# One fp32 encoder step on one core: the sample group's attention as a pipeline, and the first tiles of x, the key buffers and the last output projection in another order

## The chip, the cores and the metric

The kernel runs on one core of a Trainium2 chip. A core has a matrix engine (TensorE, PE in the profile, with PEld for its weight loads), VectorE (DVE), ScalarE (ACT), GpSimd (POOL) and SyncE (SP), which here issues every DMA. Each engine works off its own instructions strictly in the order in which they were put. The metric is the device time of one execution in microseconds (us), and a kernel's time is the median of its runs.

## The reference

17 tiles of 128 tokens go through one layer: 16 tiles of a prompt of 2048 tokens, and one tile that holds the sample group, 8 sequences of 16 new tokens with a cache of 1024 keys and values each. Everything is fp32.

```python
h = rms_norm(x, norm_g[l])
(a_x, a_b, a_c, a_z, g_q, g_f, g_i, g_z,
 s_q, s_k, s_v, s_z, m_a, m_b, m_c) = split_cols(h @ w_in[l])   # 1024 -> 15 column segments
...                      # A: gated 3-tap convolution; B: gated linear recurrence in chunks
q = rms_norm(s_q.reshape(B, T, 8, 64), q_norm_g[l])             # C: stick-breaking attention
k = rms_norm(s_k.reshape(B, T, 8, 64), k_norm_g[l])
k_all = concat([past_k, k]); v_all = concat([past_v, v])        # sample group; the prompt has no past
z = einsum('bqhd,bkhd->bhqk', q, k_all) / sqrt(64)
log_1mb = where(causal, log_sigmoid(-z), 0.0)
rest = cumsum(log_1mb, axis=3, reverse=True) - log_1mb          # from the newest key back
A = where(causal, exp(log_sigmoid(z) + rest), 0.0)
o = einsum('bhqk,bkhd->bqhd', A, v_all)
...
m = sigmoid(m_a) * (o_a @ wb[:512]) + sigmoid(m_b) * (o_b @ wb[512:1024]) + sigmoid(m_c) * (o_c @ wb[1024:])
y = x + m @ w_out[l]
```

## The kernel before

**Arithmetic.** Each fp32 operand of a large product is split into a high and a low part (`split`: a rounding cast `hi` on ACT, and `lo = src - hi` on DVE), and each product takes three matmuls, hi·hi, hi·lo and lo·hi (`PASS3`). `wload` fetches 512 KB of weights at a time into `wst` (two buffers) and splits them into `whi` and `wlo`.

**Head.** Before the first projection `first_steps` loads five tiles of x; tile 0 is the sample group. For each, ACT squares and sums a row (`square`, L505), POOL makes the reciprocal root (`rstd_of`: `rv` L195, `rr` L197), DVE scales by it and by the gain row `g_bc` (`scale`, L510), PE transposes in two halves of four 128x128 blocks (`turn`, L521), and each half is split into `hh` and `hl`. The first projection needs tiles 0 to 2. POOL also builds constants there: `qblk` and `bsel`, and the masks `mtmp`, which DVE casts into `lmask`.

**Projections.** The tiles are taken in three groups. For each, `run_jobs` walks a list of jobs, one for each weight slice; a job is a generator, and after every few matmuls it yields a cost and lets queues of other work go on by so much: `run_late` (the end of `post_qk`), `hbg` (the recurrence) and `bg`. `post_qk` takes q or k of a tile, norms it, transposes it (L700) and copies it to `kt` (L702), which one DMA writes to `KT` or `QT`; `kt` has one buffer.

**The sample group's attention** runs in `bg` during the second group, from some 624 to 1231 us. For each of 8 sequences and three segments of keys (`sg` 2, 1, 0, newest first), 24 steps in all, it loads cached keys `kc`, transposes them into `kt`, multiplies by the zero-padded queries `qz` (`z`, L412), takes two sigmoids on ACT, a scan and a product `sp` on DVE (L426), transposes `sp` on PE (L429), copies that to `at_` on ACT (L436) and multiplies it by the cached values `vc` into `pv` (L447). One step ends before the next begins. The newest segment has two cached blocks and 16 new keys, which go a path of their own.

**Prompt attention** follows in `bg` from the third group on.

**Merge.** From some 2290 us on, groups of tiles (`PGROUPS`) go through `bjob(x, dp)` for the three branches (matmuls L1225; `gate` L1233 on DVE; from the second branch on the sum `mp` on POOL, L1234; after the third `mp` is split into `mh` and `ml`), and `ojob(s)` multiplies by four slices of `w_out` (L1247) and adds x (`yt`, L1253). The output jobs of a group are put between the next group's branch jobs. The last group has four tiles, and its four output jobs have nothing left beside them.

Rows of the profile name a line, an engine, an operation, and the tiles written and read, so "L429 tp<-idf,sp" is the transposition of `sp` at line 429.

Of the kernel before, what the change touches and what calls it, by code (L numbers as in the profile page):

```python
# [16 lines left out]
P = 128  # L17
# [81 lines left out]
def trunk(ctx: ExitStack, tc: tile.TileContext, x_prompt, x_sample, cache_conv, state_hgrn, cache_k, cache_v,  # L99
# [72 lines left out]
    nc.sync.dma_start(g_bc, norm_g[0].partition_broadcast(P))  # L172

    def split(hi, lo, src, eng=None):

        nc.scalar.copy(hi, src)  # L176
        (eng or nc.vector).tensor_tensor(lo, src, hi.bitcast(F32), ALU.subtract)  # L177

    def wload(pieces):

        out = []
        for v in pieces:
            a, b = v.shape[1], v.shape[2]
            st = wp.tile([P, a, b], F32, tag="wst", name="wst", bufs=2)
            nc.sync.dma_start(st, v)
            hi = wp.tile([P, a, b], F32R, tag="whi", name="whi")
            lo = wp.tile([P, a, b], F32R, tag="wlo", name="wlo")
            split(hi, lo, st)
            out.append((hi, lo))
        return out  # L190

    def rstd_of(ssq, n, count):
# [4 lines left out]
        nc.gpsimd.tensor_tensor(r, v, mhalf.broadcast_to([P, n]), ALU.pow)  # L197
        return r
# [58 lines left out]
    def attn_pair(m0, m1):  # L257
# [15 lines left out]
        for m in range(m0, m1):  # L273
# [8 lines left out]
            for i in range(nq):  # L282
# [17 lines left out]
                if b0 > 0:  # L300
                    carry[e][i] = at.tile([P, 1], F32, tag="carry", name="carry", bufs=16)
# [42 lines left out]
    def sample_attention():  # L344
# [45 lines left out]
        for b in range(NB):  # L390
            pv = ps_pv()
            carry = one
            vnew = sa.tile([TS, 8, 64], F32, tag="vnew", name="vnew", bufs=1)
            nc.sync.dma_start(vnew, VV[b * TS:(b + 1) * TS])
            for sg in (2, 1, 0):
                nblk = 2 if sg == 2 else 3
                w = nblk * P + (TS if sg == 2 else 0)
                kt = sa.tile([P, 4, 384], F32, tag="kt", name="kt", bufs=2)
                for bi in range(nblk):
                    blk = 3 * sg + bi  # L400
                    kc = sa.tile([P, 512], F32, tag="cst", name="kc", bufs=3)
                    nc.sync.dma_start(kc, cache_k[0, b, blk * P:(blk + 1) * P].rearrange("t h d -> t (h d)"))
                    tp = ps_tp()
                    for h in range(4):
                        nc.tensor.transpose(tp[:, h * P:(h + 1) * P], kc[:, h * P:(h + 1) * P], idf)
                    nc.scalar.copy(kt[:, :, bi * P:(bi + 1) * P], tp.rearrange("p (h t) -> p h t", h=4))
                    yield 1.3
                z = ps_z()
                if sg == 2:
                    nc.tensor.matmul(z[:, 256:256 + TS], idb, nmask, start=True, stop=False, skip_group_check=True)  # L410
                for h in range(4):
                    nc.tensor.matmul(z[32 * h:32 * h + 32, :nblk * P], qz[:, h, b], kt[:, h, :nblk * P],  # L412
                                     start=sg != 2, stop=True, skip_group_check=True)
                if sg == 2:
                    for h in range(4):
                        nc.tensor.matmul(z[32 * h:32 * h + 32, 256:256 + TS], qz[:, h, b],
                                         knew[:, h, b * TS:(b + 1) * TS], start=False, stop=True,
                                         skip_group_check=True)
                nc.scalar.activation(sn[:, 384 - w:384], z[:, :w], AF.Sigmoid, scale=-0.125)
                sp = sa.tile([P, 384], F32, tag="sp", name="sp")  # L420
                nc.scalar.activation(sp[:, :w], z[:, :w], AF.Sigmoid, scale=0.125)
                pr = sa.tile([P, 385], F32, tag="pr", name="pr")
                s_in = sn[:, 384 - w:385][:, ::-1]
                nc.vector.tensor_tensor_scan(pr[:, 384 - w:385][:, ::-1], s_in, s_in, carry, ALU.mult, ALU.bypass)
                carry = pr[:, 384 - w:385 - w]
                nc.vector.tensor_tensor(sp[:, :w], sp[:, :w], pr[:, 385 - w:385], ALU.mult)  # L426
                tp = ps_tp()
                for bi in range(nblk):
                    nc.tensor.transpose(tp[:, bi * P:(bi + 1) * P], sp[:, bi * P:(bi + 1) * P], idf)  # L429
                at_ = sa.tile([P, 384], F32, tag="at", name="at_")  # L430
                if sg == 2:
                    nc.tensor.transpose(tp[0:TS, 256:384], sp[:, 256:256 + TS], idf)
                    nc.scalar.copy(at_[:, 0:256], tp[:, 0:256])
                    nc.scalar.copy(at_[0:TS, 256:384], tp[0:TS, 256:384])
                else:
                    nc.scalar.copy(at_, tp[:, :384])  # L436
                yield 2.0
                for bi in range(3):
                    blk = 3 * sg + bi
                    if blk == 8:  # L440
                        vc, n = vnew, TS
                    else:
                        vc, n = sa.tile([P, 8, 64], F32, tag="vst", name="vc", bufs=3), P
                        nc.sync.dma_start(vc, cache_v[0, b, blk * P:(blk + 1) * P])
                    for h in range(4):
                        c = bi * P + 32 * h
                        nc.tensor.matmul(pv[32 * h:32 * h + 32, 0:P].rearrange("p (e d) -> p e d", e=2),  # L447
                                         at_[0:n, c:c + 32], vc[0:n, 2 * h:2 * h + 2],
                                         start=sg == 2 and bi == 0, stop=sg == 0 and bi == 2, skip_group_check=True)
                    yield 0.6  # L450
            od = sa.tile([P, P], F32, tag="od", name="od", bufs=1)
            nc.scalar.copy(od, pv[:, 0:P])
            for h in range(8):
                nc.sync.dma_start(OCS[b * TS:(b + 1) * TS, h * 64:(h + 1) * 64],
                                  od[h * TS:(h + 1) * TS, 64 * (h % 2):64 * (h % 2) + 64])
            yield 1.0
# [24 lines left out]
    class Prepare:  # L481
# [30 lines left out]
        def turn(self, i, kk):  # L512
# [10 lines left out]
            split(hh[sl], hl[sl], tp.rearrange("p (k t) -> p k t", k=4))  # L523
# [42 lines left out]

# [74 lines left out]
    lmax = const.tile([P, 4], F32, name="lmax")  # L641
    nc.vector.tensor_copy(lmax, vec[:, 12:16])
    lexp = const.tile([P, 4], F32, name="lexp")
    nc.vector.tensor_tensor(lexp, vec[:, 12:16], lmax, ALU.subtract)
    ebase = const.tile([P, 1], F32, name="ebase")
    nc.vector.memset(ebase, 2.718281828459045)
    nc.gpsimd.tensor_tensor(lexp, ebase.broadcast_to([P, 4]), lexp, ALU.pow)
    lsum = const.tile([P, 4], F32, name="lsum")
    nc.vector.reciprocal(lsum, lexp)
    lsm = const.tile([P, 4], F32, name="lsm")  # L650
    nc.vector.tensor_tensor(lsm, lexp, lsum, ALU.mult)
    lb = const.tile([P, 4], F32, name="lb")
    nc.vector.tensor_tensor(lb, lsm, lsm, ALU.subtract)
    omlb = const.tile([P, 4], F32, name="omlb")
    nc.vector.tensor_scalar(omlb, lb, -1.0, 1.0, ALU.mult, ALU.add)
# [4 lines left out]
    for h in (1, 2, 4, 8, 16, 32, 64):  # L660
        nblk = 64 // h
        mt = g0p.tile([P, 2, 64], F32, tag="mtmp", name="mtmp", bufs=2)
        nc.gpsimd.memset(mt[:, :, :nblk], 1.0)
        for i in range(2):
            m = mt[:, i, :nblk]
            nc.gpsimd.affine_select(m, m, pattern=[[-2 * h, nblk]], base=-h * i, channel_multiplier=1,
                                    compare_op=ALU.is_ge, fill=0.0)
            nc.gpsimd.affine_select(m, m, pattern=[[2 * h, nblk]], base=h + h * i, channel_multiplier=-1,
                                    compare_op=ALU.is_gt, fill=0.0)
        lmask[h] = const.tile([P, 2 * nblk], I32, name=f"lmask{h}")  # L670
        nc.vector.tensor_copy(lmask[h].rearrange("p (i b) -> p i b", i=2), mt[:, :, :nblk])
# [632 lines left out]
```

## Time and profile before

| | |
|---|---|
| runs | median 3031.82 us (3031.12 to 3034.32, 3 runs) |
| profiled execution | 3036.76 us; its span on the core 3035.1 us |
| TensorE clock granted, mean | 0.991 of full speed |
| PE matmuls | 2934.7 us, 97% of the span, 19609 instructions |
| DVE | 1759.2 us, 58% |
| ACT | 1230.2 us, 41% |
| POOL | 454.7 us, 15% |
| DMA | 394.40 MB, 130 GB/s |

The profile shows one execution; its own time is 4.94 us above the median, so differences are worked out against 3036.76 and the result is carried to the median. PE is busy nearly throughout, and what is left on it is idle gaps and stretches where the clock of its matmuls is granted at half speed.

### The profile page before, as it was taken

How to read it: one execution, taken by the hardware profiler on the slowest of the kernel's cores; microseconds unless marked ns; L12 is line 12 of the kernel's file. 1: busy time of each engine (PE TensorE's matmuls, PEld its weight loads, DVE VectorE, ACT ScalarE, POOL GpSimd, SP SyncE). 2: the span in 40 equal slices, each digit the busy share in tenths (PEclk: the TensorE clock that was granted, in tenths of full speed). 3: DMA queues.
4: the chain of work that ended last, by engine and by line, in shares of the span. 5: the costliest groups of instructions: out<-in, count | busy, mean ns of one | idle time of the engine just before them, and what ended most of it. 6: DMA issues, size and time to landing. Idle time of an engine off the chain costs nothing. (4 is left out here: it accounts for less than half of the span.)

```text
span 3035.1 us, 51813 instructions
## 1 busy us (share of the span) xinstructions
PE 2934.7 (97%) x19609; PEld 2688.3 (89%) x19609; DVE 1759.2 (58%) x3412; ACT 1230.2 (41%) x2571; POOL 454.7 (15%) x861
## 2 busy tenths in 40 slices
PE   7999999999999999999999999999999899899998
PEld 7999999988988888999899998998998788687887
DVE  5345535652434352636635757567577877978753
ACT  4332232243333333224434444444445555555531
POOL 3110000110100000001322111111012412313211
PEclk9999999999999999999999999999999999999999
DMA  5433323455444444323444232323226455555553
GB/s 178 139 109 112 99 90 105 120 161 166 130 126 138 130 131 121 115 78 114 150 152 127 81 122 81 119 66 100 89 87 216 149 164 171 157 184 170 171 160 121
DMA packets 448842, 394.40 MB, mean 130 GB/s; under 512 B 24809, under 2 KB 388674, under 8 KB 448594
## 3 DMA queue, kind: packets, MB, share of 16 engines
q1 hardware_dynamic: 448594, 391.09, 42.3%
q8 instruction: 155, 2.54, 0.4%
q14 instruction: 93, 0.76, 0.1%
HBM read 303.67 MB, written 87.33 MB: 129 GB/s over the span
## 5 line engine op out<-in xcount | busy, mean ns | idle before, releaser
L587 PE MATMUL acc<-hh,whi 128*128 128x384 f32 (+1 forms) x2688 | 937.8, 349 | 0.5 <-ACT hh L176 0.3
L587 PE MATMUL acc<-hl,whi 128*128 128x384 f32 (+1 forms) x2688 | 887.6, 330 | 0.0
L587 PE MATMUL acc<-hh,wlo 128*128 128x384 f32 (+1 forms) x2688 | 887.5, 330 | 0.0
L177 DVE TENSOR_TENSOR wlo<-wst,whi 128x1024 fp32r<-128x1024 f32 x296 | 372.1, 1260 | 435.0 <-ACT whi L176 420.7
L587 PEld LDWEIGHTS acc<-hh,whi 128*128 128x128 f32 x2688 | 508.1, 189 | 37.3 <-issue 31.1
L587 PEld LDWEIGHTS acc<-hl,whi 128*128 128x128 f32 x2688 | 509.2, 189 | 4.9 <-issue 1.0
L587 PEld LDWEIGHTS acc<-hh,wlo 128*128 128x128 f32 x2688 | 507.3, 189 | 0.0
L176 ACT CAST whi<-wst 128x1024 fp32r<-128x1024 f32 x296 | 311.0, 1051 | 364.1 <-PE acc L587 272.4
L598 PE MATMUL acc<-whi,hh 128*128 128x256 f32 x1088 | 317.2, 292 | 7.2 <-DVE gm L986 5.0
L598 PE MATMUL acc<-wlo,hh 128*128 128x256 f32 x1088 | 308.6, 284 | 0.5 <-DVE wlo L177 0.5
L598 PE MATMUL acc<-whi,hl 128*128 128x256 f32 x1088 | 308.6, 284 | 0.0
L298 DVE TENSOR_TENSOR_SCAN pr<-snb,carry 128x513 f32<-128x513 f32 x192 | 259.4, 1352 | 74.3 <-ACT snb L289 73.2
L271 ACT COPY aT<-tp 128x512 f32<-128x512 f32 (+2 forms) x320 | 167.8, 525 | 236.3 <-PE tp L270 233.6
L303 DVE TENSOR_TENSOR sp<-sp,pr 128x512 f32<-128x512 f32 (+2 forms) x320 | 202.0, 631 | 35.1 <-POOL sp L294 13.2
L598 PEld LDWEIGHTS acc<-whi,hh 128*128 128x128 f32 x1088 | 207.2, 190 | 11.7 <-DVE gm L986 5.7
L289 ACT ACTIVATE snb<-z 128x512 f32<-128x512 f32 (+2 forms) x320 | 172.3, 539 | 90.2 <-PE z L286 85.5
L598 PEld LDWEIGHTS acc<-wlo,hh 128*128 128x128 f32 x1088 | 207.4, 191 | 0.7 <-DVE wlo L177 0.7
L598 PEld LDWEIGHTS acc<-whi,hl 128*128 128x128 f32 x1088 | 207.4, 191 | 0.4
L270 PE MATMUL tp<-idf,sp 128*128 128x128 f32 x1088 | 173.1, 275 | 15.8 <-ACT aT L271 15.1
L1225 PE MATMUL acc<-oh,whi 128*128 128x512 f32 (+2 forms) x480 | 179.8, 376 | 8.6 <-DVE gate L1233 7.1
L298 DVE TENSOR_TENSOR_SCAN pr<-snb,one 128x129 f32<-128x129 f32 (+3 forms) x128 | 114.5, 894 | 112.1 <-POOL snb L294 112.0
L291 ACT ACTIVATE sp<-z 128x512 f32<-128x512 f32 (+2 forms) x320 | 171.7, 537 | 16.9 <-DMA OX<-ot 13.0
(301 smaller groups left out, 4773.4 us busy)
## 6 DMA issues: line engine op xcount, KB each, us to landing
wst<-in_w_in_dram SPq DMA_DIRECT2D x216, 512.0 KB, 3.9
wst<-in_w_branch_dram SPq DMA_DIRECT2D x48, 512.0 KB, 4.0
GM<-gm SPq DMA_DIRECT2D x120, 192.0 KB, 2.0
Kt<-KT SPq DMA_DIRECT2D x80, 256.0 KB, 3.1
gate<-GM SPq DMA_DIRECT2D x72, 256.0 KB, 2.7
kc<-in_cache_k_dram SPq DMA_DIRECT2D x64, 256.0 KB, 2.9
vc<-in_cache_v_dram SPq DMA_DIRECT2D x64, 256.0 KB, 2.8
wst<-in_w_out_dram SPq DMA_DIRECT2D x32, 512.0 KB, 4.5
```

The source lines that it names most:

```text
L176: nc.scalar.copy(hi, src)
L177: (eng or nc.vector).tensor_tensor(lo, src, hi.bitcast(F32), ALU.subtract)
L270: nc.tensor.transpose(tp[:, j * P:(j + 1) * P], sp[:, j * P:(j + 1) * P], idf)
L271: nc.scalar.copy(aT[:, e, 0:nb, i * P:(i + 1) * P], tp[:, :w].rearrange("p (b q) -> p b q", q=P))
L289: nc.scalar.activation(sn[:, 512 - w:512], z[:, :w], AF.Sigmoid, scale=-0.125)
L291: nc.scalar.activation(sp[:, :w], z[:, :w], AF.Sigmoid, scale=0.125)
L298: nc.vector.tensor_tensor_scan(pr[:, 512 - w:513][:, ::-1], s_in, s_in, one if diag else carry[e][i], ALU.mult, ALU.bypass)
L303: nc.vector.tensor_tensor(sp[:, :w], sp[:, :w], pr[:, 513 - w:513], ALU.mult)
L587: nc.tensor.matmul(acc[:, :n], w[0][a][:, k], hT[b][:, k, :n], start=k == 0 and i == 0, stop=k == KB - 1 and i == 2)
L598: nc.tensor.matmul(acc[:, :256], hT[b][:, k, ti * P:(ti + 1) * P], w[k // 4][a][:, k % 4], start=k == 0 and i == 0, stop=k == KB - 1 and i ...
L1225: nc.tensor.matmul(acc[:, :n], w[0][a][:, k, dd * P:(dd + 1) * P], box[x][b][:, k, sl], start=k == 0 and i == 0, stop=k == 3 and i == 2)
```

## The change

- `first_steps`: `g_bc` is loaded behind the sample tile. Tiles 0 to 2 are squared, scaled and transposed, and tiles 3 and 4 only behind the first split of weights. The constants (`build_bound`, `build_masks`, `build_selectors`) are put behind the latest `rr` and the first split.
- `post_qk`: `kt` has two buffers. `carry` of the prompt attention has 9 in place of 16.
- `sample_attention`: the same arithmetic, with the next step's keys transposed ahead of this step's `turned` (transposition of the product), and the next step's scores put behind this step's `values`. Two zeroed buffers `sps` and a zeroed `vnew` of 128 partitions let all steps make three transpositions and one copy. The loads of `vc` are issued in `turned`, ahead of the job's next matmuls.
- The last group's merge: for the third branch the sum `mp` is made on DVE, and the first output job takes three tiles together, first with k 0 to 5 and then with k 6 and 7. `xr` has 3 buffers, `yt` 2.

```diff
 first_steps:
+                if i == 0:
+                    nc.sync.dma_start(g_bc, norm_g[0].partition_broadcast(P))
             for f in (self.square, self.scale):
                 for i in range(2):
                     f(i)
             for i in range(n):
                 if i > 2:
-                    self.square(i)
-                    yield
-                    self.scale(i)
-                    yield
+                    with tc.issue_after(first_split[0].ins), tc.issue_after(first_split[1].ins):
+                        self.square(i)
+                        yield
+                        self.scale(i)
+                        yield
                 for kk in range(0, KB, 4):
                     self.turn(i, kk)
                     yield
-                    if i == 0:
-                        (self.scale if kk else self.square)(2)
+                    if i == 0 and not kk:
+                        self.square(2)
+                if i == 0:
+                    with tc.issue_after(self.last[1].ins):
+                        self.scale(2)
                 self.ready = i
+                yield
 run_jobs:
+            if not g and at_ == 1:
+                with tc.issue_after(rstd_at[0].ins), tc.issue_after(first_split[1].ins):
+                    build_bound()
+                    build_masks()
+                    build_selectors()
 post_qk:
-        kt = qk.tile([P, 4, P], F32R, tag="kt", name="kt", bufs=1)
+        kt = qk.tile([P, 4, P], F32R, tag="kt", name="kt", bufs=2)
 sample_attention (after):
+        sps = [single([P, 384], F32, f"sps{i}") for i in range(2)]
+        for x in sps:
+            nc.gpsimd.memset(x, 0.0)
...
+        def turned(m):
+            b, sg = order[m]
+            sp = held[m][0]
+            tp = ps_tp()
+            for bi in range(3):
+                nc.tensor.transpose(tp[:, bi * P:(bi + 1) * P], sp[:, bi * P:(bi + 1) * P], idf)
+            at_ = sa.tile([P, 384], F32, tag="at", name="at_")
+            nc.scalar.copy(at_, tp[:, :384])
+            for bi in range(blocks(m)):
+                vc = sa.tile([P, 8, 64], F32, tag="vst", name="vc", bufs=3)
+                nc.sync.dma_start(vc, cache_v[0, b, blk * P:(blk + 1) * P])
...
+        yield from keys(0)
+        scores(0, masked(0))
+        yield 0.7
+        for m in range(last + 1):
+            if m < last:
+                yield from keys(m + 1)
+            turned(m)
+            yield 2.0
+            z = masked(m + 1) if m < last else None
+            values(m)
+            if z is not None:
+                scores(m + 1, z)
+            yield 2.2
 bjob:
-                            nc.gpsimd.tensor_tensor(m, m, gate[:, sl], ALU.add)
+                            (nc.vector if final and x == 2 else nc.gpsimd).tensor_tensor(
+                                m, m, gate[:, sl], ALU.add)
 ojob:
+            cuts = [KB - 2, KB] if final and s == 0 else [KB]
...
+                    for c, end in enumerate(cuts):
+                        for ti in some:
...
+                            for k in range(cuts[c - 1] if c else 0, end):
```

What the change moves is seen in the instructions of each engine. The first place is DVE at the start of the program. Before (`xt` with numbers are x tiles 2, 3 and 4):

```order
L510 SCALAR_TENSOR_TENSOR xt<-xt,rr,g_bc 128x1024 x2
L510 SCALAR_TENSOR_TENSOR xt_119<-xt_119,rr,g_bc 128x1024
L177 TENSOR_TENSOR hl<-tp,hh 128x4x128
L671 CAST lmask_233<-mtmp 128x128
L510 SCALAR_TENSOR_TENSOR xt_121<-xt_121,rr,g_bc 128x1024
L177 TENSOR_TENSOR hl<-tp,hh 128x4x128 x2
L671 CAST lmask_241<-mtmp 128x64
L510 SCALAR_TENSOR_TENSOR xt_123<-xt_123,rr,g_bc 128x1024
L177 TENSOR_TENSOR hl<-tp,hh 128x4x128 x2
L671 CAST lmask_249<-mtmp 128x32
L177 TENSOR_TENSOR wlo<-wst,whi 128x1024
```

After:

```order
L562 SCALAR_TENSOR_TENSOR xt<-xt,rr,g_bc 128x1024 x2
L176 TENSOR_TENSOR hl<-tp,hh 128x4x128 x2
L562 SCALAR_TENSOR_TENSOR xt_119<-xt_119,rr,g_bc 128x1024
L176 TENSOR_TENSOR hl<-tp,hh 128x4x128 x4
L694 COPY vec<-tp 128x17
L176 TENSOR_TENSOR wlo<-wst,whi 128x1024
L707 COPY lmax<-vec 128x4
L711 MEMSET ebase 128x1
L562 SCALAR_TENSOR_TENSOR xt_121<-xt_121,rr,g_bc 128x1024
L176 TENSOR_TENSOR wlo<-wst,whi 128x1024
L562 SCALAR_TENSOR_TENSOR xt_123<-xt_123,rr,g_bc 128x1024
```

Ahead of the first `wlo` there stood five scalings and three casts of masks; now there stand three scalings and no cast.

The second place is PE in one step of the sample group's attention, between the scores `z` and the transposition of their product. Before, with projections (L587) and `post_qk` (L700):

```order
L412 MATMUL z<-kt,qz 32x384 x4
L587 MATMUL acc<-hh,whi 128x384
L587 MATMUL acc<-hl,whi 128x384
L587 MATMUL acc<-hh,wlo 128x384
L587 MATMUL acc<-hh,whi 128x384
L587 MATMUL acc<-hl,whi 128x384
L587 MATMUL acc<-hh,wlo 128x384
L700 MATMUL hg<-idr,st 128x128 x4
L587 MATMUL acc<-hh,whi 128x384
L587 MATMUL acc<-hl,whi 128x384
L587 MATMUL acc<-hh,wlo 128x384
L429 MATMUL tp<-idf,sp 128x128 x3
```

After, the same engine where one step's values and the next one's scores meet:

```order
L648 MATMUL acc<-hh,wlo 128x384
L429 LDWEIGHTS idb
L429 MATMUL z<-nmask,idb 128x16
L484 MATMUL pv<-vc,at__8071 32x128 x12
L438 MATMUL z<-kt,qz 32x256 x4
L442 MATMUL z<-knew,qz 32x16 x4
L648 MATMUL acc<-hh,whi 128x384
```

Nine projection matmuls and one transposition stood between `z` and its `tp`; now the scores stand behind the step before's values, and the keys of the step after, with the work of their yields, follow ahead of `tp`: the scores `z` at position 4329 of PE's order have their `tp` (L461) at position 4438, 108 rows on.

The third place is DVE at the end of the last merge group. Before:

```order
L1233 TENSOR_TENSOR gate<-acc,gate 128x512
L177 TENSOR_TENSOR ml<-mp,mh 128x512
L1233 TENSOR_TENSOR gate<-acc,gate 128x512
L177 TENSOR_TENSOR wlo<-wst,whi 128x1024
L177 TENSOR_TENSOR ml<-mp,mh 128x512
L1253 TENSOR_TENSOR yt<-acc,xr 128x256 x3
```

After:

```order
L1308 TENSOR_TENSOR gate<-acc,gate 128x512 x2
L1309 TENSOR_TENSOR mp<-mp,gate 128x512 x2
L176 TENSOR_TENSOR ml<-mp,mh 128x512 x2
L176 TENSOR_TENSOR wlo<-wst,whi 128x1024
L1308 TENSOR_TENSOR gate<-acc,gate 128x512
L1309 TENSOR_TENSOR mp<-mp,gate 128x512
L176 TENSOR_TENSOR ml<-mp,mh 128x512
L1340 TENSOR_TENSOR yt<-acc,xr 128x256 x3
```

The sums `mp` have come into DVE's order, between `gate` and `ml`; eight of them leave POOL's.

More of the change, by code (lines that the diff above doesn't have):

```diff
@@ L171, in trunk @@
     g_bc = const.tile([P, D], F32, name="g_bc")
-    nc.sync.dma_start(g_bc, norm_g[0].partition_broadcast(P))
     def split(hi, lo, src, eng=None):
-        nc.scalar.copy(hi, src)
-        (eng or nc.vector).tensor_tensor(lo, src, hi.bitcast(F32), ALU.subtract)
+        first = nc.scalar.copy(hi, src)
+        return first, (eng or nc.vector).tensor_tensor(lo, src, hi.bitcast(F32), ALU.subtract)
+    first_split = []
     def wload(pieces):
@@ L187, in wload @@
             lo = wp.tile([P, a, b], F32R, tag="wlo", name="wlo")
-            split(hi, lo, st)
+            pair = split(hi, lo, st)
+            if not first_split:
+                first_split.extend(pair)
             out.append((hi, lo))
         return out
+    rstd_at = [None]
     def rstd_of(ssq, n, count):
@@ L389, in sample_attention @@
         yield 1.0
[L390 to L410, printed above, removed]
-                for h in range(4):
[L412 to L456, printed above, removed]
@@ new lines, in sample_attention, with blocks, keys @@
+        order = [(b, sg) for b in range(NB) for sg in (2, 1, 0)]
+        held = {}
+        pvs = {}
+        sps = [single([P, 384], F32, f"sps{i}") for i in range(2)]
+        for x in sps:
+            nc.gpsimd.memset(x, 0.0)
+        vnew = single([P, 8, 64], F32, "vnew")
+        nc.gpsimd.memset(vnew, 0.0)
+        def blocks(m):
+            return 2 if order[m][1] == 2 else 3
+        def keys(m):
+            b, sg = order[m]
+            kt = sa.tile([P, 4, 384], F32, tag="kt", name="kt", bufs=2)
+            for bi in range(blocks(m)):
+                blk = 3 * sg + bi
+                kc = sa.tile([P, 512], F32, tag="cst", name="kc", bufs=3)
+                nc.sync.dma_start(kc, cache_k[0, b, blk * P:(blk + 1) * P].rearrange("t h d -> t (h d)"))
+                tp = ps_tp()
+                for h in range(4):
+                    nc.tensor.transpose(tp[:, h * P:(h + 1) * P], kc[:, h * P:(h + 1) * P], idf)
+                nc.scalar.copy(kt[:, :, bi * P:(bi + 1) * P], tp.rearrange("p (h t) -> p h t", h=4))
+                yield 1.3
+            held[m] = [kt]
@@ new lines, in masked, with scores @@
+        def masked(m):
+            z = ps_z()
+            if order[m][1] == 2:
+                nc.tensor.matmul(z[:, 256:256 + TS], idb, nmask, start=True, stop=False, skip_group_check=True)
+            return z
+        def scores(m, z):
+            b, sg = order[m]
+            nblk = blocks(m)
+            w = nblk * P + (TS if sg == 2 else 0)
+            kt = held[m][0]
+            for h in range(4):
+                nc.tensor.matmul(z[32 * h:32 * h + 32, :nblk * P], qz[:, h, b], kt[:, h, :nblk * P],
+                                 start=sg != 2, stop=True, skip_group_check=True)
+            if sg == 2:
+                for h in range(4):
+                    nc.tensor.matmul(z[32 * h:32 * h + 32, 256:256 + TS], qz[:, h, b],
+                                     knew[:, h, b * TS:(b + 1) * TS], start=False, stop=True,
+                                     skip_group_check=True)
+            nc.scalar.activation(sn[:, 384 - w:384], z[:, :w], AF.Sigmoid, scale=-0.125)
+            sp = sps[m % 2]
+            nc.scalar.activation(sp[:, :w], z[:, :w], AF.Sigmoid, scale=0.125)
+            pr = sa.tile([P, 385], F32, tag="pr", name="pr")
+            s_in = sn[:, 384 - w:385][:, ::-1]
+            carry = one if sg == 2 else held[m - 1][1]
+            nc.vector.tensor_tensor_scan(pr[:, 384 - w:385][:, ::-1], s_in, s_in, carry, ALU.mult, ALU.bypass)
+            nc.vector.tensor_tensor(sp[:, :w], sp[:, :w], pr[:, 385 - w:385], ALU.mult)
+            held[m] = [sp, pr[:, 384 - w:385 - w]]
@@ new lines, in values @@
+        def values(m):
+            b, sg = order[m]
+            at_, vs = held[m][2:4]
+            if sg == 2:
+                pvs[b] = ps_pv()
+            pv = pvs[b]
+            for bi, vc in enumerate(vs):
+                for h in range(4):
+                    c = bi * P + 32 * h
+                    nc.tensor.matmul(pv[32 * h:32 * h + 32, 0:P].rearrange("p (e d) -> p e d", e=2),
+                                     at_[:, c:c + 32], vc[:, 2 * h:2 * h + 2],
+                                     start=sg == 2 and bi == 0, stop=sg == 0 and bi == 2, skip_group_check=True)
+            if sg == 0:
+                od = sa.tile([P, P], F32, tag="od", name="od", bufs=1)
+                nc.scalar.copy(od, pv[:, 0:P])
+                for h in range(8):
+                    nc.sync.dma_start(OCS[b * TS:(b + 1) * TS, h * 64:(h + 1) * 64],
+                                      od[h * TS:(h + 1) * TS, 64 * (h % 2):64 * (h % 2) + 64])
@@ L457, in sample_attention @@
+        last = len(order) - 1
+        yield from keys(0)
[11 more added lines that the diff above has]
+            yield 2.2
         oc = sa.tile([P, 512], F32, tag="cst", name="oc", bufs=3)
@@ L522, in turn @@
             sl = (slice(None), slice(kk, kk + 4), slice(ti * P, (ti + 1) * P))
-            split(hh[sl], hl[sl], tp.rearrange("p (k t) -> p k t", k=4))
+            self.last = split(hh[sl], hl[sl], tp.rearrange("p (k t) -> p k t", k=4))
         def steps(self):
@@ new lines, in trunk, with build_masks @@
+    lmask = {}
+    def build_masks():
+        for h in (1, 2, 4, 8, 16, 32, 64):
+            nblk = 64 // h
+            mt = g0p.tile([P, 2, 64], F32, tag="mtmp", name="mtmp", bufs=2)
+            nc.gpsimd.memset(mt[:, :, :nblk], 1.0)
+            for i in range(2):
+                m = mt[:, i, :nblk]
+                nc.gpsimd.affine_select(m, m, pattern=[[-2 * h, nblk]], base=-h * i, channel_multiplier=1,
+                                        compare_op=ALU.is_ge, fill=0.0)
+                nc.gpsimd.affine_select(m, m, pattern=[[2 * h, nblk]], base=h + h * i, channel_multiplier=-1,
+                                        compare_op=ALU.is_gt, fill=0.0)
+            lmask[h] = const.tile([P, 2 * nblk], I32, name=f"lmask{h}")
+            nc.vector.tensor_copy(lmask[h].rearrange("p (i b) -> p i b", i=2), mt[:, :, :nblk])
```

100 lines of the change are left out of this document (53 added, 47 removed).

## The prediction

> **What bounds the kernel now.** I read the page first, then PE's waits, then the stretches of half clock, and then the trace at each place that the change touches. The page gives the bound.
>
> ```profile
> span 3035.1 us, 51813 instructions
> PE 2934.7 (97%) x19609; PEld 2688.3 (89%) x19609; DVE 1759.2 (58%) x3412; ACT 1230.2 (41%) x2571; POOL 454.7 (15%) x861
> ```
>
> PE is idle for 3035.1 - 2934.7 = 100.4 us. No matmul is taken away, so the change can win part of these 100 us, and of the time that matmuls lose at half clock. PE's waits, with the tile that PE was to work on and what it waited for (total us, count, longest), name the gaps:
>
> ```profile
> PE tp L521 <- DVE xt L510: 12.5, 3, 10.9
> PE tp L429 <- DVE sp L426: 11.0, 21, 2.3
> PE hg L700 <- ACT kt L702: 7.4, 6, 2.3
> PE acc L1247 <- ACT mh L176: 5.7, 3, 2.7
> PE pv L447 <- ACT at__7899 L436: 1.0, 1, 1.0
> ```
>
> The first is the head, the second and fifth are the sample group's attention, the third is `post_qk`, the fourth is the end. Next come windows around stretches of half clock. The columns are the window, its length, busy time and count of PE, PEld, DVE, ACT and POOL, the granted clock, and the share and GB/s of the DMAs. The last row is the end, at full clock.
>
> ```profile
> 69.30:76.10 6.80, 5.80 (x29) 5.80 (x29) 2.32 (x6) 1.89 (x6) 1.20 (x2) 0.50 0.67 193
> 670.00:673.40 3.40, 3.40 (x15) 3.16 (x13) 1.09 (x3) 1.56 (x3) 0.00 (x0) 0.50 0.53 174
> 707.60:711.00 3.40, 2.68 (x9) 2.17 (x7) 0.43 (x2) 0.78 (x2) 0.00 (x0) 0.50 0.54 182
> 810.00:813.40 3.40, 3.40 (x18) 3.40 (x18) 0.42 (x1) 1.10 (x3) 0.19 (x1) 0.50 0.79 230
> 1509.70:1513.10 3.40, 3.22 (x14) 3.22 (x15) 1.24 (x4) 0.82 (x5) 0.54 (x2) 0.50 0.93 280
> 1639.40:1642.80 3.40, 3.40 (x17) 3.22 (x16) 0.24 (x1) 1.68 (x5) 0.54 (x2) 0.50 0.35 114
> 2980.80:2991.10 10.30, 7.20 (x30) 6.60 (x31) 3.54 (x5) 1.76 (x3) 2.11 (x1) 0.50 0.26 78
> 2991.10:3031.20 40.10, 40.10 (x338) 39.93 (x337) 11.71 (x19) 5.25 (x5) 0.00 (x0) 1.00 0.40 128
> ```
>
> At full clock a 256-wide matmul takes 40.10 / 338 = 0.119 us. In the first window 29 of them took 5.80 us, where 3.44 would have done. A half-clock stretch so loses 41% of its busy time.
>
> **Part 1, the key buffer.** With one `kt`, the next copy waits until the DMA has written the last one out. ACT's queue stands meanwhile, and behind it the casts and evacuations that PE wants:
>
> ```profile
> 68.91 0.59 ACT L702 CAST kt<-tp 128x512 fp32r<-128x512 f32 x1 [2.98 <-DMA KT<-kt]
> 70.30 0.58 PE L598 MATMUL acc<-whi,hh 128*128 128x256 f32 x1 [2.89 <-DVE gm L986]
> PE acc L598 <- DVE gm L986: 4.0, 2, 2.9
> PE acc L598 <- ACT vg L1054: 1.0, 1, 1.0
> PE hg L700 <- ACT kt L702: 1.3, 2, 0.8
> PE hg L700 <- ACT kt L702: 6.1, 4, 2.3
> ```
>
> The last four rows are PE's waits in 50 to 200 us (two rows), 624 to 1231 and 1420 to 1660. At 70.30 the profile names `gm`, which DVE makes after ACT, and ACT had just stood 2.98 us for the write of `kt`; so I count these rows to `kt`. Idle: 4.0 + 1.0 + 1.3 + 6.1 = 12.4 us. Clock, in the windows at 69, 1509 and 1639: (5.80 + 3.22 + 3.40) x 0.41 = 5.1 us. With two buffers a copy waits only for the write before last. **17.5 us**. Bounds: 6.1 if only the waits that name `kt` in the third group go, 17.5 if all go. I take the upper end, since the waits come where two copies stand close together. What is late next is the third copy of a row of three, 0 to 3 us, which is in the allowance below.
>
> **Part 2, the sample group's attention.** Before, a step's `z` and the transposition of its product stand nine projection matmuls and one transposition apart, and PE arrives first:
>
> ```profile
> 663.64 0.85 PE L412 MATMUL z<-kt,qz 128*32 128x384 f32 x8
> 669.51 0.55 PE L429 MATMUL tp<-idf,sp 128*128 128x128 f32 x3 [2.35 <-DVE sp L426]
> ```
>
> Nine 384-wide matmuls are 9 x 0.119 x 1.5 = 1.6 us, against a chain of two sigmoids, a scan and a product. After, some hundred matmuls stand between them where I counted, over 12 us at these prices, against the same chain; even the smallest distance that I found there, about 5 us, exceeds what was 2.35 us short. All of 11.0 + 1.0 = 12.0 us idle should go, and the half-clock stretches that follow these gaps: (3.40 + 2.68 + 3.40) x 0.41 = 3.9 us. **15.9 us**, bounds 10 (a third of the waits stay) and 20 (the grouped `pv` and `z` matmuls, some 4 us of further small gaps). The instructions added cost PE nothing: 8 sequences lose one copy on ACT each (-8), and a longer multiplication by `vnew` has the same columns; POOL's three memsets stand ahead of the first step. Their cover is that ACT and DVE are busy 41% and 58% of the span.
>
> The added waits are in SP's queue: the loads of `vc` now stand in `turned`, behind whatever weight load waits there.
>
> ```profile
> 1501.81 3.10 SPq L185 DMA_DIRECT2D wst<-in_w_in_dram  x2
> vc<-in_cache_v_dram SPq DMA_DIRECT2D x64, 256.0 KB, 2.8
> ```
>
> A pair of weight loads held SP for 3.1 us in the first row, and 2.8 us from issue to landing follow by the second; between `turned` and `values` PE's order has some 3.4 us of other work at the least (20 projection matmuls of 384 columns at 0.178). I allow one late `vc` in eight steps, some 1 us in sum, within the allowance below.
>
> **Part 3, the head.**
>
> ```profile
> 6.42 1.06 ACT L505 ACTIVATE junk<-xt 128x1024 bf16<-128x1024 f32 x1 [4.36 <-DMA xt<-in_x_sample_dram]
> 7.78 1.06 ACT L505 ACTIVATE junk<-xt 128x1024 bf16<-128x1024 f32 x1 [0.20 <-DMA xt<-in_x_prompt_dram]
> 7.90 1.06 POOL L809 MEMSET qblk<- 128x1152 f32 x1
> 8.93 0.57 POOL L197 TENSOR_TENSOR rr<-rv,mhalf 128x1 f32<-128x1 f32 x1
> 9.53 1.28 DVE L510 SCALAR_TENSOR_TENSOR xt<-xt,rr,g_bc 128x1024 f32<-128x1024 f32 x1 [7.59 <-POOL rr L197]
> 10.87 1.97 PE L521 MATMUL tp<-idf,xt 128*128 128x128 f32 x8 [10.87 <-DVE xt L510]
> 15.18 0.68 DVE L177 TENSOR_TENSOR hl<-tp,hh 128x512 fp32r<-128x512 f32 x1
> 21.30 2.00 ACT L176 CAST whi<-wst 128x1024 fp32r<-128x1024 f32 x2
> 22.38 1.23 DVE L177 TENSOR_TENSOR wlo<-wst,whi 128x1024 fp32r<-128x1024 f32 x1
> 22.56 0.67 PE L587 MATMUL acc<-hh,whi 128*128 128x384 f32 x1
> ```
>
> Two loads of 512 KB in sequence were used 7.78 - 6.42 = 1.36 us apart, so the sample tile ahead of `g_bc` lands about 1.4 us earlier (bounds 0 and 1.4). The memset of 1.06 us between `rv` and `rr` is gone. The first scaling starts at 9.53 - 2.4 = 7.1. Its first half reaches `hl` at 7.1 + 1.28 + 1.0 (PE) + 0.59 (`hh`, as its twin `kt` above) + 0.68 = 10.7. With two transposition buffers the five further halves follow at (1.0 + 0.59 + 0.68) / 2 = 1.13 us each, with one scaling between: 17.6. `whi` runs on ACT from about 16.7, and the first matmul starts at about 17.8 in place of 22.56, 4.8 us earlier. From this I take 0.6, since the first `wlo` (1.23) ends later than PE comes to it. **4.2 us**, bounds 2 (POOL's deferred masks hold a cast that stands ahead of tile 4's `hl` on DVE) and 6. The two scalings of tiles 3 and 4 cost DVE 2.56 us behind the first split, under the second chunk's cover of 24 matmuls per job.
>
> **Part 4, the end.**
>
> ```profile
> 2974.00 0.69 DVE L1233 TENSOR_TENSOR gate<-acc,gate 128x512 f32<-128x512 f32 x1
> 2974.83 2.13 POOL L1234 TENSOR_TENSOR mp<-mp,gate 128x512 f32<-128x512 f32 x1 [2.12 <-DVE gate L1233]
> 2976.99 0.62 ACT L176 CAST mh<-mp 128x512 fp32r<-128x512 f32 x1 [2.67 <-POOL mp L1234]
> 3031.67 0.42 DVE L1253 TENSOR_TENSOR yt<-acc,xr 128x256 f32<-128x256 f32 x1 [1.98 <-DMA out_dram<-yt]
> PE acc L1225 <- DVE gate L1233: 1.0, 1, 1.0
> ```
>
> From the last branch matmul's end at 2974.4 to 3031.2 PE needs 56.8 us for 4 x 4 x 24 = 384 matmuls, which at 0.119 are 45.5: 11.3 us lost to waits for `mh` and to half clock (the window at 2980.80). After, the sum costs DVE 0.69 a time (as `gate`, a product of two such tiles, in the first row) in place of POOL's 2.13: the last tile is split at 2974.0 + 4 x 0.69 = 2976.8, and the first output job, with three tiles of k 0 to 5, gives PE 3 x 18 x 0.119 = 6.4 us of work until 2980.8. The slack is 4 us. DVE now carries 3 x 0.69 + 1.23 / 2 = 2.7 us for each d, against 24 x 0.119 = 2.85 on PE: it keeps pace, narrowly. With the wait for `gate` in the last row (1.0, from 2940 on) and 0.4 from the second `yt` at the end: **12.7 us**, bounds 7 (DVE falls behind PE by 0.7 us a time) and 13.
>
> **The sum.** 17.5 + 15.9 + 4.2 + 12.7 = 50.3. I take off 3 us (bounds 0 and 8) for what is late next: the third `kt`, a late `vc`, a mask. The gain is 47 us: 3036.8 becomes 2989.5 in the profiled execution, and the median, which is 4.9 below it, 3031.8 - 47 = **2985 us**. The other waits (the middle, from 1660 to 2940 us) stay as they are, since there the same instructions follow each other on every engine. About 0.2%, 6 us, is what a measurement can tell from no change.
>
> **The rivals.**
>
> *The clock does not come back.* The stretches at half clock may not hang on the gaps that go. Then 5.1 + 3.9 us stay and so do some 3 of the tail's: gain 47 - 12 = 35, time 2997. Against it: at 669.51 a gap of 2.35 us is followed at once by the window at 670 with clock 0.50, and the 2.89 us at 70.30 lie in the window at 69.30. The Trainium skill, "TensorE: Matmul & The Clock Gate", section "What's actually happening", has the clock halved after an idle window of about 3.4 us; by that rule gaps below 3 us would halve nothing, and removing them would give no clock back. The trace disagrees, with 0.50 behind 2.35 us. Chance 0.14.
>
> *The sample group's steps still wait.* PE might come too early for `kc` or `vc`, so that the 15.9 us only change their name: time 2985 + 16 = 3001. For it: SP's queue, above. Against it: the order on PE has 5 us or more at each place. Chance 0.13.
>
> *Slower.* Each of the 24 steps now needs its `vc` at one point, while before the loads stood one by one among the matmuls. If every load came behind a waiting `wst` and PE stood for it, the price is up to 3.1 + 2.8 - 3.4 = 2.5 us at a step, and at 47 / 24 = 2.0 us it eats the whole gain. At 2.5 it is 60 us: 3031.8 - 47 + 60 = 3045. Against it: 24 steps in 607 us are 25 us each, and SP is not bound to PE's place: it issues a load as soon as one of three `vst` is free. Chance 0.04. That the gaps all go elsewhere, so that nothing changes, has 0.03: PE's order shows them covered.
>
> **How the numbers follow.** The forecast has 0.66; the rivals 0.14, 0.13, 0.04 and 0.03. With all terms at their upper ends the gain is 17.5 + 20 + 6 + 13 = 56.5 and a few us of small gaps: 2972 as the low end. At the high end stand 2997 and 3001 of the first two rivals with the terms' spread: 3004. Outside lie the last two cases, 0.07, and some 0.1 where several terms come out at their ends together. The likeliest case alone has 2975 to 2994. Faster by over 0.2%: 0.66 + 0.14 + 0.13 = 0.93; the same 0.03; slower 0.04.
>
> **What would show it.** Of the changed kernel: PE's waits for `sp` (11.0) and `kt` (7.4) under 2 us each; no clock of 0.50 near 70, 670, 1510 and 1640 us; the first projection matmul at 18 us; no POOL row between `gate` and `mh` at the end, and no more than 47 us from the last branch matmul to the last output matmul; the sample stage at 591 rather than 607 us. I am wrong if ACT still waits for the write of `kt`, if PE waits for `vc`, or if DVE is behind at the end, which a wait of PE for `ml` would show.

## The result and the profile after

The changed kernel takes 2956.61 us (median; 2950.41 to 2957.01), the kernel before on the same chip 3031.47: a ratio of 0.9747 (95% interval 0.973 to 0.9764), 75 us less. I forecast 2985 (2972 to 3004): the sign was right, the gain was 1.6 times the forecast, and the time lies below the range. One execution each of two later kernels took far longer than the others (5716.4 us with the head alone, 13343.71 us with the version that beats both), and the ratios leave these two out. The profiled execution took 2956.66 us. The page after:

```profile
span 2955.0 us, 51793 instructions
PE 2891.1 (98%) x19609; PEld 2685.5 (91%) x19609; DVE 1762.7 (60%) x3420; ACT 1228.4 (42%) x2563; POOL 438.2 (15%) x856
```

PE does the same 19609 matmuls. Its idle time fell from 100.4 to 63.9 us, and its busy time by 43.6 us: more than half of the gain comes from time that the profile calls busy. PE's longest waits after:

```profile
PE tp L275 <- ACT aT L276: 10.4, 6, 3.1
PE tp L573 <- DVE xt L562: 10.4, 4, 8.2
PE acc L1300 <- DVE gate L1308: 6.2, 6, 1.6
```

The waits for the sample group's `sp` (11.0 us before), for the `kt` of `post_qk` (7.4) and for `mh` (5.7) are gone from the list, and no wait for `vc` or `ml` has come into it; `aT` and `gate` belong to the prompt attention and the merge. ACT's own waits for the write of `kt`, 54.3 and 28.1 us before, are

```profile
ACT kt L768 <- DMA QT<-kt: 4.1, 2, 2.2
ACT kt L768 <- DMA KT<-kt: 1.7, 2, 1.4
```

The first scaling and the first projection, and three rows of the end, a sum and the split behind it:

```profile
6.83 1.28 DVE L562 SCALAR_TENSOR_TENSOR xt<-xt,rr,g_bc 128x1024 f32<-128x1024 f32 x1 [4.96 <-POOL rr L202]
18.03 0.69 PE L648 MATMUL acc<-hh,whi 128*128 128x384 f32 x1 [0.79 <-ACT whi L175]
...
2893.88 0.69 DVE L1309 TENSOR_TENSOR mp<-mp,gate 128x512 f32<-128x512 f32 x1
2894.61 0.62 ACT L175 CAST mh<-mp 128x512 fp32r<-128x512 f32 x1 [2.44 <-DVE mp L1309]
2895.26 0.69 DVE L176 TENSOR_TENSOR ml<-mp,mh 128x512 fp32r<-128x512 f32 x1 [0.69 <-ACT mh L175]
```

To see where the time went, I cut both traces at the same matmuls of the projections and the merge, whose order among themselves is the same. The second group's stretch runs from the 3601st of these matmuls to the 6601st, which takes in the sample group's attention but for its last few us after the change; the third runs from there to the first matmul of the merge. What each stretch became shorter, in the two profiled executions, beside the terms of the prediction put to the same stretches (an own table, from the starts of matmuls):

| stretch | measured, us | predicted, us |
|---|---|---|
| up to the first projection matmul | 4.5 | 4.2 |
| first group | 10.3 | 7.4 |
| second group, with the sample group's attention | 45.1 | 17.2 |
| third group | 8.8 | 8.8 |
| merge up to its last group's third branch | -1.1 | 0 |
| end | 12.0 | 12.7 |

All but one are within 3 us, and the second group holds nearly the whole error. How closely the others agree is in part luck: this one trace of the kernel before is long. The traces of the six experiments below that leave the third group as it was are 2.9 to 5.1 us shorter there, those that leave the first group as it was 0.4 to 2.3, and the end 1.2 to 1.7. The second group's stretch before and after (columns as in the prediction, PE alone):

```profile
603.10:1231.90 628.80, 611.00 (x4548) 0.99 0.46 136
```

```profile
588.30:1172.00 583.70, 579.62 (x4546) 1.00 0.48 146
```

Idle fell from 17.8 to 4.1 us, 13.7, about what I had counted (12.0 and 1.3). Busy fell by 31.4, of which the clock can explain a few us. The rest must be matmuls that take less time in another company. In the trace before, one block of the value product stands among projections like this (start, length, PE's rows):

```profile
776.72 0.28 PE L598 MATMUL acc<-whi,hl 128*128 128x256 f32 x1
776.84 0.28 PE L598 MATMUL acc<-wlo,hh 128*128 128x256 f32 x1
777.04 0.43 PE L447 MATMUL pv<-vc,at__8580 128*32 128x128 f32 x8
777.40 0.39 PE L598 MATMUL acc<-whi,hh 128*128 128x256 f32 x1
777.62 0.28 PE L598 MATMUL acc<-whi,hl 128*128 128x256 f32 x1
777.74 0.28 PE L598 MATMUL acc<-wlo,hh 128*128 128x256 f32 x1
```

Projections start 0.12 us apart. Around the block the steps are 0.20, 0.36 and 0.22: from 776.84 to 777.62 0.78 us pass, 0.54 more than two projections need, and no row shows idle time, because a row's length reaches over the next one's start. The weight loads (PEld) show what happens at the two borders:

```profile
776.72 0.19 PEld L598 LDWEIGHTS acc<-wlo,hh 128*128 128x128 f32 x1
777.04 0.16 PEld L447 LDWEIGHTS pv<-vc,at__8580 128*32 128x32 f32 x8
777.40 0.19 PEld L598 LDWEIGHTS acc<-whi,hh 128*128 128x128 f32 x1 [0.20 <-issue]
777.51 0.19 PEld L598 LDWEIGHTS acc<-whi,hl 128*128 128x128 f32 x1
```

Among projections, the weights of the next matmul start to load some 0.12 us ahead of it (776.72 for 776.84), while the one before runs. Into the block and out of it, the load starts only with its own matmul, at 777.04 and 777.40. Over all 45 blocks of that form the median was 0.554 us, for a block of scores 0.985 (11 blocks). After, the value product's twelve matmuls (24 rows' worth) and the scores stand in one block:

```profile
771.93 0.33 PE L648 MATMUL acc<-hh,wlo 128*128 128x384 f32 x1
772.19 0.86 PE L484 MATMUL pv<-vc,at__8900 128*32 128x128 f32 x24
772.87 0.83 PE L438 MATMUL z<-kt,qz 128*32 128x384 f32 x8
773.63 0.44 PE L648 MATMUL acc<-hh,whi 128*128 128x384 f32 x1
773.91 0.34 PE L648 MATMUL acc<-hl,whi 128*128 128x384 f32 x1
```

That costs 1.638 us (median of five) where 3 x 0.554 + 0.985 = 2.647 were paid: 1.01 us a step, 24 us over the 24 steps. Four blocks became one, so going in and out of a block costs (2.647 - 1.638) / 3 = 0.336 us. By contrast blocks of three and four 128x128 transpositions cost 0.330 and 0.439 us, and six rows of the recurrence's 128x128 products and transpositions 0.666: 0.11 a row, with nothing for going in and out. That is the theory to be tested: the price belongs to the switch between 128-column and 32-column matmuls. Its rival: the pipeline removed waits that the profile does not show. The Trainium skill, "TensorEngine Tiling (Array Packing)", section "Key Properties", says that a change of the tiling mode drains TensorE, and gives no figure; the prices here agree, with about 0.17 us for each of two changes.

### The profile page after: what moved, and what is told of

It is laid out like the page before. It is cut to its first block, busy times and chain, and to the rows that moved or that the text cites. A ratio compares the mean times of both kernels' runs of the same rounds, so it can differ in the third digit from the quotient of the medians.

```text
span 2955.0 us, 51793 instructions
## 1 busy us (share of the span) xinstructions
PE 2891.1 (98%) x19609; PEld 2685.5 (91%) x19609; DVE 1762.7 (60%) x3420; ACT 1228.4 (42%) x2563; POOL 438.2 (15%) x856
## 3 DMA queue, kind: packets, MB, share of 16 engines
q1 hardware_dynamic: 448594, 391.09, 43.3%
## 5 line engine op out<-in xcount | busy, mean ns | idle before, releaser
L275 PE MATMUL tp<-idf,sp 128*128 128x128 f32 x1088 | 172.9, 275 | 15.9 <-ACT aT L276 10.4
```

Source lines behind the costliest of these rows:

```text
L275: nc.tensor.transpose(tp[:, j * P:(j + 1) * P], sp[:, j * P:(j + 1) * P], idf)
```

## The experiments

**The pipeline alone**: the kernel before with the new `sample_attention` only.

> The kernel before with the sample group's pipeline alone. The sample stage took 45 us less in the changed kernel. If the stage carries that by itself, the time is 3031.5 - 45 = 2986 (2980 to 2992). My prediction's own term was 15.9 us: 3015. A rival is that part of the 45 us came from the second key buffer, whose copies share ACT with the stage: then 2990 to 3000.

Ratio 0.9889 (0.9874 to 0.9904), 33.6 us; the stage took 594.6 us, 34.2 less than before. So the pipeline carries three quarters of the stage's gain, over twice what I had put down for it. The rival of the expectation is right about the rest, a part needs the key buffer: in this trace PE waits 6.1 us in the stage for `kt` of `post_qk`, where it waited 1.3 before.

**The second key buffer alone** (`kt` with two, and `carry` with 9 to make room).

> The kernel before with the second key buffer (and the smaller ring of carries that makes room for it) alone. Prediction's term: 17.5 us, 3014. From where the changed kernel gained time in the first and third group: 6 to 8 + 2.7 + 8.4 = 17 to 19 us, 3012 to 3014. Rival: the waits only move to the next write, 6 us, 3025.

Ratio 0.9923 (0.9911 to 0.9935): 23 us, more than any of the expectations. The first and third group gained 10.1 and 11.2 us against the long trace before, and the prediction had 7.4 and 8.8. The surprise is the second group:

```profile
592.90:1212.60 619.70, 606.22 (x4550) 1.00 0.45 138
```

9.1 us less than the 628.8 before: three half-clock stretches went (about 4 us), the waits for `kt` (1.3), and 2.0 of the 11.0 us for `sp`, whose sigmoids stand behind `kt` on ACT. With 34.2 from the pipeline this makes 43.3 of 45.1.

**Grouping without the pipeline.**

```diff
                     for h in range(4):
                         ...
-                    yield 0.6
+                yield 1.8
```

> The kernel before, not pipelined, but the three blocks of a step's value product stand together (12 matmuls in a row in place of three times 4), everything else as before. Theory of the switch: each block of 32-column matmuls between projections costs PE about 0.336 us for going in and out; 2 x 24 of these go, 16 us: 3015. Theory of waits: all of the stage's gain comes from the pipeline, grouping brings nothing or makes PE wait for the value tiles: 3028 to 3040.

Ratio 0.9971 (0.996 to 0.9983), 8.8 us, and the stage became 10.2 us shorter:

```profile
600.70:1219.30 618.60, 597.59 (x4549) 0.99 0.45 139
```

Busy time fell by 13.4 us, near the 16 expected; idle time rose from 17.8 to 21.0. PE's waits show what is late next:

```profile
PE tp L429 <- DVE sp L426: 11.0, 21, 2.4
PE hg L700 <- ACT kt L702: 3.4, 2, 2.1
PE pv L447 <- ACT at__7899 L436: 2.2, 1, 2.2
```

So grouping pays without a pipeline, against the theory of waits, but some 3 us of it come back as waits for `kt` and `at_`, to which PE now comes earlier. The trace also gives the price a second time: a block of 24 rows of the value product costs 0.98 us there and one of 8 rows 0.55, so 0.027 a row and 0.33 for the block.

**The pipeline without grouping.** The three blocks and the scores stand apart again.

```diff
+                yield 0.6                  # in values, behind each block
...
-            z = masked(m + 1) if m < last else None
-            values(m)
-            if z is not None:
-                scores(m + 1, z)
-            yield 2.2
+            yield from values(m)
+            if m < last:
+                scores(m + 1, masked(m + 1))
+            yield 0.4
```

> The changed kernel with its pipeline, but the value product's three blocks and the next scores stand apart again, with projections between them. Theory of the switch: 3 x 24 x 0.336 = 24 us slower than the changed kernel, 2981 against 2957. Theory of waits: the same as the changed kernel within 4 us, since nothing waits more.

2976.61 us, ratio 0.9833 (0.982 to 0.9847) against 0.9747 for the change. The stage:

```profile
589.30:1194.30 605.00, 600.38 (x4533) 1.00 0.46 141
```

605.0 against 583.7, 21.3 us more, with nearly the same idle time as after (4.6 and 4.1); by the ratios, which come from two chips, the whole is 26 us slower. Nothing waits noticeably more; the same matmuls are only spread out. This is the theory of the switch, with 21 for 24 us.

**One switch more.** The value product stays together, and the scores stand a few projections behind it.

```diff
-            z = masked(m + 1) if m < last else None
             values(m)
-            if z is not None:
-                scores(m + 1, z)
-            yield 2.2
+            yield 0.6
+            if m < last:
+                scores(m + 1, masked(m + 1))
+            yield 1.6
```

> The changed kernel with the value product's twelve matmuls still together, but the next scores put a few projection matmuls behind them. Theory of the switch: one more block of 32-column matmuls in each of 23 steps, 23 x 0.336 = 8 us more in the sample stage (the three splits together cost 21 us there). Theory of waits: no difference, since the scores still stand far ahead of what needs them.

2960.28 us, ratio 0.9768 (0.9755 to 0.9781). The change itself on the same chip:

> The changed kernel once more, beside the two that follow. Same ratio to the kernel before as at first, 0.9747 (0.973 to 0.9764).

2950.85 us, ratio 0.9737 (0.9724 to 0.975). The difference is 9.4 us, and between the stages (591.4 and 582.4 us) 9.0; expected were 8. Taking one switch apart costs 0.4 us a step, taking three apart 0.9. The price of the switch is shown, in both directions and in two sizes. That it is not the shorter runs of projections rests on the 128-column transpositions and products that pay nothing.

Which property of the 32-column blocks costs it is less clear; I tried no kernel that changes the columns of these matmuls alone, but two groups of rows in the trace before bear on it. The prompt attention's value product has 64 columns (L315), and its matmuls start in pairs. Twelve of its blocks, 16 rows of 512, cost 3.78 us in the median, and twelve others, four rows each of 512, 384, 256 and 128, cost 2.50: 8192 against 5120 columns in all, so 0.42 us a thousand columns and 0.36 us for the block. It pays like the 32-column blocks. A single narrow matmul does not: from the start of a 16-column transposition (L432) to the second projection behind it 0.286 us pass in seven of eight cases, which is what a 128-column transposition (0.11) and a projection (0.18) need. So few columns alone don't cost. The blocks that pay are those whose matmuls run side by side, in pairs there and in fours here (the first four rows of the block at 777.04 start within 0.02 us); that this is the property is read from these rows and was not tested.

**The head alone.**

> The kernel before with the head's new order alone. Prediction's term: 4.2 us (2 to 6), 3027; the changed kernel's first projection stood 4.5 us earlier. Rival: what comes after the first projection (masks, tiles 3 and 4 put later) gives part of it back: 3030.

Ratio 0.9993 (0.9984 to 1.0002), 2 us, not told from no change. The interval reaches from 5 us faster to 0.6 slower, so it doesn't rule out the 4.2 of the prediction. In its trace the first projection starts 4.5 us earlier, as in the changed kernel. At the end of the first group the trace is still 2.9 to 4.9 us ahead of the five traces with the old head and one key buffer, so at most some 1.6 us are given back by then; what comes later these runs can't tell.

**The end, whole and in halves.**

> The kernel before with the new end alone (sum on DVE, first output job cut, more buffers). Prediction's term: 12.7 us, 3019; the changed kernel gained 12.4 us there.

> Of the new end only the sum of the last group's third branch on DVE; output jobs and buffers as before. The chain gate to mh gets 2.13 - 0.69 = 1.4 us shorter, and POOL's queue of sums goes: if the wait for mh was POOL's rate, 8 to 12 us of 12.4 come from here, 3021; if the order of the output job carries it, 2 to 4 us, 3028.

> Of the new end only the cut of the first output job (three tiles with k 0 to 5 first) and the buffers; the sum stays on POOL. PE has 6.4 us of work before it needs the last two slices, which came at 2977 + 1.3 and later: 8 to 12 us, 3021. If POOL's backlog is longer than 6.4 us, less: 4 to 6 us, 3026.

The ratios are 0.9977 (0.9968 to 0.9986), 0.9978 (0.9969 to 0.9986) and 0.9991 (0.9982 to 1.0): 7, 7 and 3 us. In the traces the end is 12.0, 12.2 and 7.4 us shorter than in the trace before; that one trace is on the long side there, since four kernels with the old end (pipeline, key buffer, grouping and head alone) were 1.2 to 1.7 us shorter as well. The last branch's stretch, before and after:

```profile
2925.50:2995.50 70.00, 62.40 (x303) 0.93 0.49 153
```

```profile
2857.90:2915.40 57.50, 57.50 (x303) 1.00 0.59 183
```

No idle time and no half clock is left. The sum on DVE does it alone; the cut alone leaves PE small waits, and cutting on top of the sum brings nothing that shows.

**A version that beats both.** After the change ACT still waits for POOL's sums in the first three merge groups (`mh` for `mp`: 73.1 us in all), with the prompt attention's `aT` behind it in the queue. The same edit for all four groups:

```diff
-                            (nc.vector if final and x == 2 else nc.gpsimd).tensor_tensor(
+                            (nc.vector if x == 2 else nc.gpsimd).tensor_tensor(
```

> The changed kernel with the sum of the third branch on DVE in all four merge groups, not in the last alone. In the changed kernel ACT's casts mh wait 1.4 to 2.7 us for POOL's sums near 2351 to 2359 us, and PE waits 6.0 + 3.1 us for copies aT that stand behind them on ACT. If these go: 9 us and up to three half-clock windows of 1.4 us, 9 to 13 us less in the merge stage. Rival: DVE, which carries the prompt attention's scans there, gets 24 x 0.69 = 17 us more work and PE waits for it: 0 to 10 us more.

2932.84 us, ratio 0.9675 (0.9661 to 0.9688) to the kernel before, 18 us better than the change on the same chip (0.9737). Its trace is that of one more execution.

> The kernel with the sum on DVE in all four merge groups again, for its trace: its time should lie at 2931 to 2938, with the gain of some 18 us between 2290 and 2880 us of the changed kernel, PE's waits for aT (10.4 us) down to 2 or less, and fewer half-clock windows there (five in the changed kernel's trace).

2934.99 us. PE's waits in the merge and the attention:

```profile
PE tp L275 <- ACT aT L276: 6.1, 2, 5.7
PE acc L1300 <- DVE gate L1308: 3.7, 4, 1.3
PE pv L320 <- ACT aT L276: 2.7, 2, 2.4
PE z L290 <- ACT sp L296: 1.4, 3, 0.7
```

The merge up to its last group's third branch became 18 us shorter than after the change (617.8 against 636.1), with three half-clock windows in place of five. The waits for `aT` did not fall to 2 us as expected, but from 10.4 to 6.1, one of 5.7 being left; `sp` went from 5.5 to 1.4 and `gate` from 6.2 to 3.7. DVE's 17 us more of work cost PE nothing that shows; DVE's busy time in that stretch even stays the same (510.53 and 510.36 us), for its other instructions became shorter without POOL's sums beside them. Two groups of DVE in this stretch (busy time, mean ns of one), after the change and in this version:

```profile
L176 DVE TENSOR_TENSOR wlo<-wst,whi 128x1024 fp32r<-128x1024 f32 x62 | 86.2, 1390 | 2.0 <-ACT whi L175 1.6
L176 DVE TENSOR_TENSOR ol<-ost,oh 128x512 fp32r<-128x512 f32 x35 | 28.8, 826 | 1.7 <-ACT oh L175 1.7
```

```profile
L176 DVE TENSOR_TENSOR wlo<-wst,whi 128x1024 fp32r<-128x1024 f32 x61 | 78.5, 1286 | 2.5 <-ACT whi L175 2.3
L176 DVE TENSOR_TENSOR ol<-ost,oh 128x512 fp32r<-128x512 f32 x35 | 23.9, 684 | 4.5 <-ACT oh L175 4.5
```

The trace after the change shows by itself that it is POOL's sums: of the 35 splits `ol`, six took 1.18 to 1.77 us, and each of these had a sum `mp` on POOL at the same time; all others took 0.66 to 0.77.

## Why the prediction was wrong, and where it was right

**The step that failed** is in part 2: the bound "10 (a third of the waits stay) and 20 (the grouped `pv` and `z` matmuls, some 4 us of further small gaps)". I had seen that the change puts these matmuls together, and gave it at most 4 us. It is worth 21 us (the pipeline with the blocks apart) to 24 (their prices), and it is not gaps at all but time in which PE counts as busy. The rows to price it were in the trace before: steps of 0.20, 0.36 and 0.22 us around a block between projections 0.12 apart. I looked for waits, and PE's busy time hides this price. The 47 us plus these 21 are 68, and the range, up to 60 us of gain, was built on a bound that no row supported.

**The waits of the sample stage** were right: idle 13.7 us less, against 13.3 counted, no wait for `sp`, none for `vc`; the smallest distance from a step's scores to its `tp` is 6.8 us, where I had found 5. The stage without grouping gained 23.8 us against 17.2. The three half-clock stretches that went there are in the 17.2 already, so 6.6 us of busy time stay open. A part may be the trace before, since four kernels that leave this stage as it was had it up to 3.3 us shorter; the rest I can't place.

**The key buffer** was right in its places (first and third group 19.1 us, against 16.2, of which the long trace before gives some us), but in the second group I counted only what names `kt`. The sign that was to show me wrong, that ACT still waits for the write of `kt`, came in small: 5.8 us are left of 82.4. On its own it brought 23 us against 17.5, since it also freed ACT for the sample stage, which then hands `sp` over sooner.

**The head**: 6.83 and 18.03 us against 7.1 and 17.8, right by its steps. **The end**: right in the trace (12.0 against 12.7), though the long trace gives 1.2 to 1.7 of it, and though two edits were summed where one suffices; the runs alone show 7 (4 to 10).

**The allowance** of 3 us for late buffers was hardly needed; the merge lost 1.1. **The rivals**: the clock did come back, with 8 half-clock windows of 3.4 us inside the span after the change against 16 before. The sample steps do not wait, and no value tile is late, though the loads take longer to land (3.6 us against 2.8). In the rival called slower a product is off: 20 matmuls at 0.178 are 3.6 us and not 3.4, which makes 2.3 us a step in place of 2.5; nothing else hung on it.

## What to carry to other kernels

Before adding up idle time, look at the steps between the starts of instructions on the engine that bounds: what a matmul of another shape costs among its neighbours stands there and nowhere in its busy share. Price a regrouping by these steps, group by group, before calling it small. And where one engine's queue holds two users' work, a wait that is taken from one of them also pays in the other's stage, so look for it there.

## What the runs showed of the hardware

**The switch.** A block of 32-column matmuls between 128-column ones costs about 0.34 us beyond its own work, at full clock, and one of 64-column matmuls 0.36; 128-column transpositions and products in the same place cost nothing extra, nor did a single 16-column transposition.

**DVE beside POOL.** The same split `ol` takes 826 ns on average with POOL's sums in the stretch and 684 ns without, `wlo` 1390 and 1286. Single ones are hit: up to 1.77 us, against 0.68 to 0.69 with POOL at rest.

**The clock has a grid.** This was shown only by the traces together; no kernel was made for it. In all traces half-clock stretches are multiples of 3.413 us, and they start on a grid of that step from the first full clock on. Over 13 traces I counted PE's busy share in each window of the grid that ran at full clock: of 81 under 0.47, 79 were followed by a half-clock window; of 86 between 0.47 and 0.6, 8; of some 11000 above 0.6, none. So not the length of a gap decides but how much of one window it fills. (The Trainium skill, "TensorE: Matmul & The Clock Gate", section "What's actually happening", has a free-running window of about 3.4 us, and the length agrees; that the window has to be idle does not, since half busy is little enough.) Three windows of the kernel before, PE alone, and two of the kernel with one switch more:

```profile
666.60:670.00 3.40, 1.05 (x8) 1.00 0.96 239
670.00:673.40 3.40, 3.40 (x15) 0.50 0.53 174
673.40:676.80 3.40, 3.40 (x32) 0.99 0.78 215
```

```profile
2535.10:2538.50 3.40, 1.78 (x8) 1.00 0.90 313
2538.50:2541.90 3.40, 1.86 (x10) 1.00 0.51 157
```

In the first, 2.35 us of idle lie in one window, which is busy for 31%, and the next one runs at half speed, with 15 matmuls where 32 go at full clock. In the second a gap of 3.2 us falls across a border of the grid, both windows are busy for over half, and the clock stays. Where a gap falls changes with everything ahead of it; a window costs, by the 41% that the prediction worked out, 3.4 x 0.41 = 1.4 us (an estimate), and the kernel before had 16 such windows in its trace, the changed one 8 in its first trace and 4 in its second. That is as large as several of the terms above, and it can be one reason why runs of one kernel here lie up to 14 us apart. Of the runs that were only timed the record has the mean granted clock: over the kernel before, 33 runs on one chip, it went from 0.992 to 0.997, and lower clocks went with longer times (correlation -0.63). On the other chip 9 runs between 0.992 and 0.994 show no such order.
